# The planner that orders a streaming encoder step estimates a matmul with a larger fixed part and a smaller minimum

## The chip, the cores and the metric

The kernel runs on one core of one Trainium2 chip. The metric is the device time of one execution in microseconds; the median of three runs of the kernel before is 1734.06 us. Engines are named as the profile names them: PE (matmuls), PEld (its weight loads), DVE, ACT, POOL, and SP, which here only issues DMAs.

## The reference

One layer of a hybrid encoder, for 2064 prompt positions (16 learned ones and 2048 given) and 8 short streams of 16 positions that have 256 cached positions each. All is float32.

```python
h = rmsnorm(x, norm_g)
q, k, v, za, logf, bg, u, zc = project(h, w_in, b_f)     # one 1024 x 4104 projection, u = C * h_c
# 8 heads of 64, in blocks of 128 queries; c is the running sum of logf
s = einsum('bqhd,bkhd->bhqk', qblk, k) * DH ** -0.5 + cq - ck
p = softmax(where(kpos <= qpos, s, -inf))
o_a = einsum('bhqk,bkhd->bqhd', p, v)
y_c = bg * causal_conv(u_full, conv_w)                   # depthwise, width 3
x = x + concat(o_a * silu(za), y_c * silu(zc)) @ w_out
y = rmsnorm(x, final_g)                                  # k, v, logf and the last u are outputs too
```

## The kernel before

Every float32 product is made of matmuls on halves: a value is split into a rounded high half and a low remainder (`hh` and `hl` of the normalised tokens, `wh` and `wl` of the weights, `ph` and `pl` of the softmax weights), and three products (high by high, low by high, high by low) add up in PSUM.

**Stages.** Positions are worked on in two groups: 1280 prompt positions with the short streams, and then the other 784. A group is normalised, transposed and projected; its attention runs in between the projections and the convolution, since these need no softmax. Between the two groups the short streams have their own attention, and after the second come the output projection and the last norm.

**A projection** takes a weight of 1024 x 128: `raw` is loaded by a DMA that ACT issues (one buffer), ACT rounds it to `wh`, DVE subtracts to `wl` (two buffers each), and each column tile of the group takes 24 matmuls into a PSUM tile `ps`. A column tile is 256 or 384 wide in the first group and 256 or 272 in the second. Keys and queries leave through the tiles `eh` and `el`, one buffer each (`EB = 1`), and SP stores them to `kh_d`, `kl_d`, `qh_d`, `ql_d` in DRAM.

**Attention** goes by head and by units of 256 queries: five units a head in the first group, three in the second. `scores_of` makes the score tiles `sp` from the query tiles `qa`, `qb` (two of each) and the key tiles `ka`, `kb`, copies them to a row `s` and exponentiates it; `weights_of` transposes the row into `tp` and splits it into `ph` and `pl`; `values_of` adds up `o` (one buffer) from these and from `vb`, the values of the head. `vb` has one buffer, so the load of the next head's values can start only when the last `o` matmul of this head is done. The gate `gz` is multiplied in by POOL, and the result is stored to `cat_d`.

**What sets the order.** All of this is written as generators, the streams `v` (values), `w` (weights), `s` (scores) and the main one (projections or convolution). `weave` steps one of them at a time: the first in the order of priority whose next step has its data by the planner's clock, `self.pe + SLACK`; attention stands ahead of the main stream. That clock is the sum of what `cost` says of every matmul that has been placed, so `cost` sets where attention and projections alternate. PE runs in the order in which the generators were stepped. The orders of DVE, ACT, POOL and SP are sorted by the times that the same planner works out (`note`, `place`, `settle`), and SP issues its DMAs strictly in that order: one that waits holds up those behind it. No instruction is added or left out by `cost`.

```python
                t = s[1]()
                if t <= self.pe + self.SLACK:
                    best = s
                    break
```

Of the kernel before, what the change touches and what calls it, by code (L numbers as in the profile page):

```python
# [67 lines left out]
class Times:  # L68
# [17 lines left out]
    def cost(self, queue, op, out, k):  # L86
        cols = 1
        for x in out.shape[1:]:
            cols *= x
        if queue == "tensor":  # L90
            if op == "transpose":
                return 109.0
            four = k["rhs"].dtype == F32
            return max(214.0 if four else 107.0, cols * (4 if four else 1) / 2.4) + 2.0
        if queue == "gpsimd":
            if k.get("op") == ALU.pow:
                return 464.0
            if op == "partition_all_reduce":
                return 472 + 6.25 * cols
            return 60 + 0.68 * cols if op == "memset" else 115 + 2.2 * cols  # L100
        if queue == "scalar":
            far = k["in_"].tensor.name.rsplit("_", 1)[0] not in WHOLE
            return 52 + 48 * far + 0.83 * cols + 95 * ("accum_out" in k or "bias" in k)
        if op == "tensor_scalar" and "accum_out" in k:
            return 220 + 1.05 * cols
        if op in ("tensor_copy", "tensor_scalar"):
            return 60 + 0.55 * cols + 60 * ("scalar1" in k and not isinstance(k["scalar1"], float))
        if op == "tensor_reduce":
            cols = 1
            for x in k["in_"].shape[1:]:  # L110
                cols *= x
        return 60 + 60 * (op == "scalar_tensor_tensor") + 1.05 * cols

    def place(self, queue, ready, cost):
        if queue == "tensor":
            self.pe = max(self.pe, ready) + cost
            return self.pe
        iv = self.busy.setdefault(queue, [])
        while iv and iv[0][1] < self.pe - 30000.0:
            iv.pop(0)  # L120
        at = max(ready, self.pe - 30000.0)
        k = 0
        while k < len(iv):
            if iv[k][1] > at:
                if iv[k][0] >= at + cost:
                    break
                at = iv[k][1]
            k += 1
        iv.insert(k, (at, at + cost))
        return at + cost  # L130
# [1489 lines left out]
```

## Time and profile before

| what | value |
|---|---|
| median of 3 runs | 1734.06 us (1729.77 to 1741.93) |
| the profiled execution's own time | 1732.57 us |
| its span in the trace | 1730.8 us |
| busy of the span: PE, DVE, ACT, POOL | 91%, 51%, 36%, 13% |
| matmuls | 10311 |
| issued by SP: DMA issues of `vb` | 24, for 16 heads of the two groups |

The profile is of one execution. Its ends of matmuls are modelled, so that the distance between the starts of neighbouring matmuls is what tells a matmul's price, and "idle" of PE is time in which not even the modelled end of a matmul reaches. A time of an instruction in brackets is the idle time of its engine ahead of it, with what ended it.

### The profile page before, as it was taken

Reading aid. Unit: us, or ns where it says so; the run is one execution under the profiler, and the core shown is the slowest. Engines: PE = TensorE matmul, PEld = TensorE weight load, DVE = VectorE, ACT = ScalarE, POOL = GpSimd, SP = SyncE. Lnnn points to the kernel's source line nnn. Section 1 sums busy time; section 2 is a strip of 40 time slices with the busy share of each in tenths; the row PEclk is TensorE's granted clock in tenths of the full one; section 3 lists DMA queues with packets and bytes.
Section 4 is the critical chain, followed back from the end, with each engine's and each line's share of the span. In section 5 each row is a group of like instructions: output and inputs, shape, how many; then the busy total and the mean of one; then the engine's idle time right before and its main releaser. Section 6 shows DMA issues by size and latency. Waiting matters only on the chain.

```text
span 1730.8 us, 27628 instructions
## 1 busy us (share of the span) xinstructions
PE 1578.8 (91%) x10311; PEld 1462.5 (84%) x10311; DVE 881.1 (51%) x2276; ACT 629.2 (36%) x1196; POOL 232.9 (13%) x320
## 2 busy tenths in 40 slices
PE   4977899989889899989995789999999999979998
PEld 4877889989889888989984779989889889968876
DVE  4424566526657566624321547667667657313443
ACT  4323445415435242421110435445545445312111
POOL 2200112100001120121020001000110101112222
PEclk9988999989999999999997889999999999989999
DMA  6454544364542386432136444446533413254443
GB/s 165 161 138 107 136 111 120 99 162 112 138 104 65 108 287 216 131 94 50 42 80 130 110 108 118 120 101 160 129 77 76 104 41 72 64 191 158 130 125 122
DMA packets 222241, 206.03 MB, mean 119 GB/s; under 512 B 26036, under 2 KB 196060, under 8 KB 220444
## 3 DMA queue, kind: packets, MB, share of 16 engines
q1 hardware_dynamic: 160748, 173.34, 34.0%
q10 hardware_dynamic: 61360, 30.94, 10.2%
q8 instruction: 81, 1.33, 0.3%
q14 instruction: 52, 0.43, 0.1%
HBM read 137.28 MB, written 66.93 MB: 118 GB/s over the span
## 4 chain that ended last, share of the span: by engine, by line
PE 59%; DMA 22%; DVE 5%; SPq 4%; issue 3%; ACT 3%; POOL 2%; ACTq 0%; POOLq 0%; DVEq 0%
PE ps L278 33%; PE sp L278 9%; PE o L278 9%; PE tp L278 7%; DMA raw<-in_w_in_dram 4%; SPq L278 4%; DMA cr<-cat_d 4%; DVE oxt L278 2%; DMA vb<-v_d 2%; PE tr L278 2%; DMA qh_d<-eh 1%; DMA qb<-ql_d 1%; DMA kb<-kh_d 1%; DMA gz_d<-kf 1%; DMA sqk_d<-el 1%
## 5 line engine op out<-in xcount | busy, mean ns | idle before, releaser
L278 PE MATMUL ps<-hh,wh 128*128 128x256 f32 (+2 forms) x1568 | 502.7, 321 | 23.6 <-DVE el L278 22.8
L278 PE MATMUL ps<-hl,wh 128*128 128x256 f32 (+2 forms) x1568 | 486.3, 310 | 0.0
L278 PE MATMUL ps<-hh,wl 128*128 128x256 f32 (+2 forms) x1568 | 486.0, 310 | 0.0
L278 PEld LDWEIGHTS ps<-hh,wh 128*128 128x128 f32 x1568 | 302.8, 193 | 34.1 <-DVE el L278 23.9
L278 PEld LDWEIGHTS ps<-hl,wh 128*128 128x128 f32 x1568 | 302.5, 193 | 1.8
L278 PEld LDWEIGHTS ps<-hh,wl 128*128 128x128 f32 x1568 | 301.5, 192 | 0.0
L278 DVE TENSOR_TENSOR pl<-tp,ph 128x512 fp32r<-128x512 f32 (+2 forms) x360 | 199.3, 564 | 121.3 <-ACT ph L278 117.7
L278 ACT CAST ph<-tp 128x512 fp32r<-128x512 f32 (+2 forms) x360 | 171.7, 486 | 224.4 <-PE tp L278 204.6
L278 DVE TENSOR_SCALAR_CACHE_REDUCE s<-sp 128x384 f32<-128x384 f32 (+3 forms) x360 | 211.4, 598 | 50.4 <-PE sp L278 48.8
L278 ACT ACTIVATE s<-s,nm 128x128 f32<-128x128 f32 (+16 forms) x136 | 170.5, 1254 | 84.4 <-DVE nm L278 81.9
L278 PE MATMUL tp<-ident,s 128*128 128x128 f32 (+1 forms) x1224 | 196.4, 272 | 5.0 <-DVE pl L278 5.0
L278 PE MATMUL o<-ph,vb 128*128 128x256 f32 (+4 forms) x584 | 169.8, 310 | 16.5 <-DMA vb<-v_d 11.4
L278 PEld LDWEIGHTS tp<-ident,s 128*128 128x128 f32 (+1 forms) x1224 | 148.5, 142 | 29.1 <-issue 20.9
L278 PE MATMUL sp<-kb,qb 68*128 68x384 f32 (+3 forms) x360 | 144.7, 402 | 24.2 <-DMA qb<-ql_d 20.5
L278 PE MATMUL o<-pl,vb 128*128 128x256 f32 (+4 forms) x584 | 151.2, 285 | 2.0 <-DVE pl L278 1.9
L278 POOL TENSOR_TENSOR gz<-gz,otmp 64x256 f32<-64x256 f32 (+1 forms) x64 | 47.1, 737 | 702.2 <-DVE otmp L278 629.5
L278 PE MATMUL sp<-ka,qa 128*128 128x384 f32 (+3 forms) x360 | 133.7, 371 | 0.0
L278 PEld LDWEIGHTS o<-ph,vb 128*128 128x128 f32 (+1 forms) x584 | 111.7, 191 | 23.9 <-DMA vb<-v_d 12.0
L278 PE MATMUL ps<-o,ch 128*128 128x512 f32 x374 | 118.9, 399 | 11.1 <-ACT ch L278 8.9
L278 PEld LDWEIGHTS o<-pl,vb 128*128 128x128 f32 (+1 forms) x584 | 112.4, 192 | 3.3 <-DVE pl L278 2.6
L278 PEld LDWEIGHTS ps<-o,ch 128*128 128x128 f32 x374 | 70.6, 191 | 29.7 <-ACT ch L278 9.3
L278 DVE TENSOR_TENSOR wl<-raw,wh 128x1024 fp32r<-128x1024 f32 x56 | 69.3, 1238 | 47.5 <-ACT wh L278 47.3
(193 smaller groups left out, 2080.5 us busy)
## 6 DMA issues: line engine op xcount, KB each, us to landing
raw<-in_w_in_dram ACTq DMA_DIRECT2D x59, 512.0 KB
cr<-cat_d SPq DMA_DIRECT2D x17, 512.0 KB
v_d<-vv SPq DMA_DIRECT2D x32, 256.0 KB
vb<-v_d SPq DMA_DIRECT2D x8, 1024.0 KB
oxt<-in_x_prompt_dram SPq DMA_DIRECT2D x16, 512.0 KB
out_dram<-oxt SPq DMA_DIRECT2D x16, 512.0 KB
xt<-in_x_prompt_dram SPq DMA_DIRECT2D x15, 512.0 KB
qa<-qh_d SPq DMA_DIRECT2D x112, 64.0 KB
```

The lines of the kernel that those rows point to most:

```text
L278: r = f(*a, **k)
```

## The change

One line of `cost` for a matmul that isn't a transpose. A matmul of 128 columns counted as 109 ns and counts as 65.3 now; 256 columns 108.7 and 118.7; 272 columns 115.3 and 125.3; 384 columns 162.0 and 172.0; 512 columns 215.3 and 225.3. Transposes stay at 109.

```diff
@@ -91,7 +91,7 @@
             if op == "transpose":
                 return 109.0
             four = k["rhs"].dtype == F32
-            return max(214.0 if four else 107.0, cols * (4 if four else 1) / 2.4) + 2.0
+            return max(214.0 if four else 58.0, cols * (4 if four else 1) / 2.4 + 12.0)
         if queue == "gpsimd":
```

The program holds the same instructions in another order. Three places of it follow, each before and then now.

PE, around the first value matmuls of the first group (the first rows with `o`; `ps` with `wh_1186` is the keys of the second pair of heads, `sp` are scores). Before:

```order
L278 MATMUL ps_1459<-hh1_132,wl_1187 128x384
L278 MATMUL sp_1507<-kb0_1019,qb1_1025 128x384
L278 MATMUL sp_1507<-ka0_1017,qa1_1023 128x384
...
L278 MATMUL sp_1522<-kb0_1019,qb1_1025 128x512
L278 MATMUL sp_1522<-ka0_1017,qa1_1023 128x512
L278 MATMUL sp_1522<-mask_82,identr_83 128x128
L278 MATMUL ps_1531<-hh2_134,wh_1186 128x384
...
L278 MATMUL tr_1538<-ident_77,kf_1514 128x128 x3
L278 MATMUL o_1545<-ph_1345,vb_1021 128x256
L278 MATMUL o_1545<-pl_1346,vb_1021 128x256
```

Now, the same place:

```order
L278 MATMUL sp_1440<-ka0_1017,qa0_1022 128x384
L278 MATMUL sp_1440<-mask_82,identr_83 128x128
L278 MATMUL ps_1430<-hh0_130,wh_1186 128x256
...
L278 MATMUL sp_1459<-kb0_1019,qb1_1025 128x384
L278 MATMUL sp_1459<-ka0_1017,qa1_1023 128x384
...
L278 MATMUL ps_1430<-hh0_130,wl_1187 128x256
L278 MATMUL o_1483<-ph_1332,vb_1021 128x256
L278 MATMUL o_1483<-pl_1333,vb_1021 128x256
```

The first values now stand within the first column tile of those keys (`hh0`) and not within the third (`hh2`): 117 matmuls lay between the first score and the first value matmul, and 91 do now; the first score itself stands 12 matmuls earlier.

SP, around the load of the fifth head's values in the second group (`vb_9636`, two DMAs; `qa`, `qb` are the next unit's queries, `cat_d` the store of the fourth head's last unit). Before:

```order
L278 DMA gz_13512<-gz_d2_113 64x256
L278 DMA qa0_9637<-qh_d2_94 64x272 x2
L278 DMA qb0_9639<-ql_d2_98 64x272
L278 DMA qb0_9639<-c_d_119 1x2x128 x2
L278 DMA cat_d_117<-gz_13114 64x272
L278 DMA vb_9636<-v_d1_109 128x16x128
L278 DMA vb_9636<-v_d1_109 16x128
```

Now:

```order
L278 DMA gz_13293<-gz_d2_113 64x256
...
L278 DMA qh_d3_95<-eh_13180 128x256
L278 DMA ql_d3_99<-el_13182 128x256
L278 DMA vb_9636<-v_d1_109 128x16x128
L278 DMA vb_9636<-v_d1_109 16x128
L278 DMA cat_d_117<-gz_12953 64x272
L278 DMA qa0_9637<-qh_d2_94 64x272 x2
L278 DMA qb0_9639<-ql_d2_98 64x272
L278 DMA qb0_9639<-c_d_119 1x2x128 x2
```

The load of the values now stands ahead of the five query loads and of the store, at this and at the six other head changes of the second group. On PE, 77 to 81 matmuls lay between the last value matmul of a head and the first of the next at these seven places, and 56 to 67 do now, with one of 76.

SP, around the load of the second head's values in the first group (`kh_d`, `kl_d`, `sqk_d` are stores of projected keys out of `eh` and `el`). Before:

```order
L278 DMA vb_1021<-v_d0_108 128x10x128
L278 DMA gz_2030<-gz_d0_111 64x256
L278 DMA qa1_1023<-qh_d0_92 64x256 x2
L278 DMA qb1_1025<-ql_d0_96 64x256
L278 DMA qb1_1025<-c_d_119 1x2x128 x2
L278 DMA qh_d1_93<-eh_2093 128x384
```

Now:

```order
L278 DMA vb_1021<-v_d0_108 128x10x128
L278 DMA kh_d1_101<-eh_1981 128x256
L278 DMA sqk_d_115<-eh_1981 128x128
L278 DMA kl_d1_105<-el_1983 128x256
L278 DMA sqk_d_115<-el_1983 128x128
L278 DMA out_2_dram<-st_2012 128x2x128
```

Stores out of `eh` and `el` now follow this load directly. Before, they followed in that way at the sixth head's load, where now the next queries stand in between; the seventh head's load has stores of queries behind it now too. At the end of the second group, 188 matmuls lay between the last value matmul and the first of the output projection, and 468 do now. The output stage, from its first load on, has one and the same order on SP.

## Rows read from the trace of the kernel before

**Rows 1.** The page's first part: busy time, share of the span, instructions.

```profile
PE 1578.8 (91%) x10311; PEld 1462.5 (84%) x10311; DVE 881.1 (51%) x2276; ACT 629.2 (36%) x1196; POOL 232.9 (13%) x320
```

**Rows 2.** Busy time by stretch, with the granted clock and DMA share.

```profile
core 0: us, PE busy (x) PEld busy (x) DVE busy (x) ACT busy (x) POOL busy (x), PEclk, DMA share, GB/s
0.00:110.00 110.00, 75.46 (x510) 71.69 (x510) 48.97 (x127) 39.60 (x74) 26.31 (x45) 0.95 0.56 147
110.00:590.00 480.00, 438.30 (x2963) 427.90 (x2963) 256.26 (x770) 196.87 (x407) 44.39 (x65) 0.95 0.44 114
590.00:720.00 130.00, 121.81 (x744) 111.93 (x745) 81.44 (x176) 42.77 (x87) 20.30 (x59) 0.96 0.69 227
720.00:965.00 245.00, 204.70 (x1321) 198.50 (x1320) 77.05 (x180) 45.55 (x83) 32.82 (x40) 0.92 0.37 84
...
1050.00:1500.00 450.00, 448.02 (x3267) 408.42 (x3266) 288.98 (x797) 225.00 (x412) 43.57 (x60) 1.00 0.39 94
1500.00:1731.00 231.00, 210.31 (x961) 171.36 (x960) 78.18 (x78) 39.71 (x61) 56.08 (x42) 0.97 0.44 143
```

**Rows 3.** PE's waits: total us, times, longest.

```profile
PE sp L278 <- DMA qb<-ql_d: 20.5, 6, 10.2
...
PE o L278 <- DMA vb<-v_d: 11.4, 4, 8.8
```

**Rows 4.** The chain that ended last, in order of time: start, us, what.

```profile
801.63 60.51 PE ps L278 x381
...
1503.68 13.98 PE ps L278 x114
```

**Rows 5.** PE's timeline: start, us, instruction.

```profile
304.55 0.22 PE L278 MATMUL o<-ph,vb 128*128 128x128 f32 x1
304.61 0.28 PE L278 MATMUL o<-pl,vb 128*128 128x128 f32 x1
...
820.01 0.34 PE L278 MATMUL ps<-hh,wh 128*128 128x384 f32 x1
...
821.05 0.34 PE L278 MATMUL ps<-hh,wh 128*128 128x384 f32 x1
```

**Rows 6.** Timeline at the first scores and values of the first group, PE and SP.

```profile
134.47 0.30 PE L278 MATMUL sp<-kb,qb 68*128 68x128 f32 x1 [1.32 <-DMA qb<-c_d]
...
144.64 0.46 SPq L278 DMA_DIRECT2D vb<-v_d  x1
...
161.43 0.58 PE L278 MATMUL o<-ph,vb 128*128 128x256 f32 x1 [8.82 <-DMA vb<-v_d]
161.81 0.42 PE L278 MATMUL o<-pl,vb 128*128 128x256 f32 x1
```

**Rows 7.** Timeline at the fifth head change of the second group, SP.

```profile
1296.46 1.12 SPq L278 DMA_DIRECT2D qa<-qh_d  x2
...
1300.14 2.51 SPq L278 DMA_DIRECT2D vb<-v_d  x2
```

**Rows 8.** The same place on PE: last value matmul of one head, first of the next.

```profile
1295.52 0.25 PE L278 MATMUL o<-pl,vb 16*128 16x16 f32 x1
...
1307.18 0.36 PE L278 MATMUL o<-ph,vb 128*128 128x256 f32 x1 [0.49 <-DMA vb<-v_d]
```

**Rows 9.** Timeline at the sixth head's load in the first group, SP, ACT, PE.

```profile
436.78 0.53 SPq L278 DMA_DIRECT2D vb<-v_d  x1
437.39 0.62 SPq L278 DMA_DIRECT2D kh_d<-eh  x1
...
447.13 0.38 ACT L278 ACTIVATE eh<-ps 128x256 fp32r<-128x256 f32 x1 [8.10 <-DMA kh_d<-eh]
...
449.33 0.58 PE L278 MATMUL o<-ph,vb 128*128 128x256 f32 x1 [5.16 <-DVE otmp L278]
```

**Rows 10.** The chain's weight loads, start and us.

```profile
31.32 6.51 DMA raw<-in_w_in_dram
...
226.40 10.02 DMA raw<-in_w_in_dram
```

**Rows 11.** Instructions of tile wh: min, median and max ns, first and last start.

```profile
L278 ACT CAST wh<-raw x56: 1034/1049/1074, 28.9 to 1500.3; 128x1024 fp32r<-128x1024 f32 x56
L278 DVE TENSOR_TENSOR wl<-raw,wh x56: 1206/1225/1853, 30.0 to 1502.7; 128x1024 fp32r<-128x1024 f32 x56
```

## The prediction

> **What bounds the kernel now.** I read the page's first part, then the busy time by stage, then what PE waits for. PE is busy for 91% of the span, with DVE next at 51% [rows 1], so the floor is PE's work, and only its waits and a slowed clock can be won or lost. The stages differ [rows 2]. In the second group's attention (1050 to 1500) PE is busy 448.0 of 450 us at a granted clock of 1.00: nothing is to be won there. In the first group's attention (110 to 590) it is busy 438.3 of 480: 41.7 us idle, at a clock of 0.95. Start-up (34.5 us idle of 110), the change of groups (40.3 of 245) and the output stage (20.7 of 231) have waits of their own. The waits that the order could touch end on DMAs: queries 20.5 us in 6 times, values 11.4 us in 4 [rows 3].
>
> **Which estimate is nearer.** Six 384-column matmuls in a row take 821.05 - 820.01 = 1.04 us, 173 ns each [rows 5]; the old table says 162, the new one 172. Two 128-column ones start 60 ns apart [rows 5]; old 109, new 65. The run of 381 at 801.63 takes 158.8 ns a matmul and that of 114 at 1503.68 takes 122.6 [rows 4]; with tiles of 256 and three of 384, and of 256, 256 and 272, the old table gives 148.7 and 110.9, the new one 158.7 and 120.9. So the planner's clock will now be right where it ran 6 to 10% slow. The DMA side of its estimate is left as it was.
>
> A rule speaks against that: the Trainium skill, TensorE: Matmul & The Clock Gate, section Back-to-back issue gap, gives columns/2.4 + 2.5 ns for a warm matmul, which is the old table. The trace differs (173 against 162.5 ns at 384 columns). By the page, a stretch of 58 matmuls would hide some 0.6 us less than I reckon below, so 4 us over the seven head changes would come on top of my sum.
>
> **The change, part by part.** Nothing is added or removed; 10311 matmuls stay, so PE's work is the same to within small changes of neighbours. What moves is attention against projections. A planner's clock that runs faster finds attention's data ready after fewer matmuls, and attention has priority: it stands earlier, with fewer matmuls as cover for every transfer. Before, the slow clock gave each transfer some 8% of cover that nobody planned; that is gone now. The start-up and the output stage keep their orders but for a few rows: 0.
>
> First values. The first score runs at 134.47 and the first value matmul at 161.43, after waiting 8.82 us for `vb`, which SP issued at 144.64 [rows 6]. Without that wait 117 matmuls took 18.1 us, 0.155 each; 91 take 14.1, and the first score stands 12 matmuls (2 us) earlier. PE arrives 6 us sooner at a load that SP issues three rows, about 1.5 us, sooner: the wait grows by 4.5 us. The 4.5 us of projections that slipped behind are cover for later waits on queries, which may give most of it back: between 0 and +6, I take +3, nearer the row's own wait since the later covers shrink too.
>
> The restart after that wait is slow as well: 0.38 us from the first value matmul to the second [rows 6], against 0.12 by the run of 114. It is the half clock (1.2 of 2.4 GHz) that shows in the 0.95; a longer wait pays it no second time, an additional one does, some 1 us.
>
> Stores behind a load. At 436.78 SP issued `vb`, at 437.39 a key store out of `eh`; ACT, which needs `eh` again, sat until 447.13, its queue holds the copy that frees `o`, and PE waited 5.16 us for it [rows 9]. This pattern leaves the sixth head's load and comes to the second and the seventh. One such place more is +5.2; that none bites is -5.2, that both do for long +10. The second head's load already costs PE something now (11.4 less 8.8 us of values' waits are 2.6 at three other places [rows 3]), part of which goes: I take +2.
>
> The Trainium skill, DMA: Bandwidth & Descriptors, section Queues, rings and completion order, says that each DMA engine consumes the descriptors of one ring in order. The row agrees: the store issued 0.6 us behind the load held its buffer for 9.7 us.
>
> Head changes of the second group. 1307.18 - 1295.52 = 11.7 us lie between the values of two heads [rows 8], for 81 matmuls, 0.144 each with the 0.49 wait. The load is issued 4.6 us after the last value matmul, behind five query loads and a store, and lands 7.0 us later [rows 7, 8]. Now 56 to 67 matmuls, 8.1 to 9.6 us, are the cover (76 at one place), but those six DMAs stand behind the load. If it is issued 0.5 us after the last value matmul, it needs 7.5: hidden. Between 0 and the rival below; I take +1 for all seven. What is queued behind the load is the queries of a unit that PE comes to later by more than one unit.
>
> The tail. 468 matmuls, not 188, follow the last values: over six weights in a row with nothing between them. A weight's 72 matmuls take 72 x 122.6 = 8.8 us [rows 4]. The next weight comes round in load + cast + subtract: 6.5 + 1.05 + 1.23 = 8.8 us by the shortest load on the chain, 10.0 + 2.3 = 12.3 by a longer one [rows 10, 11]. With a lead of 8.8 - 2.3 = 6.5 us, five turns at 12.3 lose 5 x 3.5 - 6.5 = 11 us, at 8.8 none. In the tail the DMA queues are calm, so the shorter row is nearer: +0.5.
>
> The short streams and everything else: idle of 8.2 us in 590 to 720 [rows 2], mostly waits for single-buffered loads whose order is shuffled. It can go or double; also the query waits can fall by as much. I take -1, between -8 and +8.
>
> Sum: 3 + 2 + 1 + 0.5 - 1 = +5.5 us on the profiled execution's 1732.57: 1738. That execution lies 1.5 us below the median of the runs, well inside their spread, so I round down to 1737.
>
> **Rivals.** (1) Slower: the value load is late all the same. If the row that SP stands at when the last value matmul is done still waits (a store whose `el` isn't written, say), the old lag of 4.6 us stays, the need is 11.6 us against 8.1 of cover, and six of the seven head changes cost 3.5 us each: +21, with the sum's other terms 1758. It decides from a lag of 1.1 us up. For it: cover was just used up before (0.49 us of wait at the fifth change [rows 8]). Against it: the six DMAs that made the lag stand behind now.
> (2) Faster: right prices place attention better, and half of the 41.7 us of idle in the first group's attention goes: -21, 1712. For it: the planner was wrong by up to a half for 128 columns. Against it: those waits end on DMAs [rows 3], whose estimates stay as they were, and covers there get shorter (70 to 58, 70 to 66, 63 to 55, 58 to 54 matmuls at four head changes).
> (3) The tail becomes bound by weight loads: +11, with the rest 1748. Against it: the calm queues.
> (4) The change does nothing: within 2 us of 1732. The order did move nearly everywhere, but PE's floor holds either way, so this differs from my forecast only in size.
>
> **How the numbers follow.** Forecast with its bounds (1726 to 1748, which takes in rival 4) 0.60; rival 1 or several bad stores 0.16; rival 2 0.16; rival 3 0.08. One per cent (17 us) is about what a measurement of this kernel can tell from no change: faster means under 1717, slower over 1751. Of rival 1 nearly all is slower, of rival 3 a third, of the forecast 0.03: 0.21. Faster: most of rival 2, 0.15. Within: 0.64. The range leaves out a tenth at each side: 1713 to 1759.
>
> **What would show it.** In the new profile: the first value matmul waits 13 us for `vb`; ACT waits for a store out of `eh` behind the second and seventh loads and no more behind the sixth; in the second group SP issues `vb` within 1 us of the last value matmul and PE doesn't wait for it; the stretch of pure projection at the end is some 60 us long and PE idles little in it; PE's idle time in the first group's attention is 42 to 50 us. I am wrong if the idle time in the first group's attention falls below 30 us, or if head changes of the second group show waits of over 2 us.

## The result, and the profile after

The change makes the kernel slower: 1765.53 us, the median of 4 runs (1745.14 to 1767.9), against 1734.85 for the kernel before (1729.77 to 1741.93). The ratio is 1.0151, with a 95% interval of 1.0114 to 1.0188. I had forecast 1737 and a range up to 1759. One of the four executions took 1745.14 us, at a mean granted clock of 0.960; the other three took 1764 us and more, at 0.947 to 0.950.

The profiled execution took 1766.87 us. Its page's first part shows PE's share down by one point and the other engines' busy times within 2 us of those before [rows 1]:

```profile
span 1765.0 us, 27666 instructions
PE 1595.8 (90%) x10311; PEld 1476.6 (84%) x10311; DVE 880.9 (50%) x2276; ACT 631.1 (36%) x1196; POOL 232.0 (13%) x320
```

PE's instructions are the same 10311, yet they are busy for 17 us more. Busy time by stretch shows where. From the second row on I cut the new trace at about the matmuls at which [rows 2] are cut, so that each row holds the same amount of PE's work (stretch, its length, the engines' busy time and instructions, granted clock, DMA share, GB/s):

```profile
0.00:110.00 110.00, 77.25 (x519) 73.65 (x520) 50.04 (x129) 40.26 (x75) 26.06 (x45) 0.95 0.59 154
110.00:587.00 477.00, 434.41 (x2957) 424.63 (x2956) 259.45 (x774) 195.94 (x406) 47.15 (x68) 0.95 0.46 117
587.00:728.00 141.00, 127.43 (x744) 115.88 (x743) 79.02 (x172) 44.59 (x90) 19.43 (x57) 0.91 0.60 194
728.00:977.00 249.00, 203.97 (x1324) 198.02 (x1323) 76.36 (x178) 44.37 (x81) 30.07 (x39) 0.92 0.40 87
...
1053.00:1536.00 483.00, 467.36 (x3263) 422.89 (x3262) 284.14 (x791) 224.04 (x410) 44.71 (x63) 0.95 0.38 88
1536.00:1765.00 229.00, 209.44 (x964) 171.76 (x962) 79.00 (x80) 39.66 (x61) 56.63 (x42) 0.97 0.45 145
```

The first group's attention takes 477 us in place of 480, with 42.6 us of idle time in place of 41.7. The short streams take 141 in place of 130. The second group's attention, of which I had written that nothing is to be won there, is where the time went: its granted clock was 1.00 before [rows 2] and is 0.95 now, and the same matmuls, but for four, take 483 us where they took 450. Its PE is busy 19 us longer and idle 14 us longer. The 85 us ahead of it (965 to 1050 before) became 76, so over the whole group, from matmul 5517 to number 9519, the first of the output projection, it is 595.7 us in place of 571.4: 24.3 of the 34.2 us between the two spans.

PE's waits in that stretch are few (who waited for whom, us in total, times, longest):

```profile
PE tp L278 <- DVE pl L278: 9.4, 4, 4.8
PE ps L278 <- DVE kf L278: 3.0, 2, 1.7
PE o L278 <- DMA vb<-v_d: 1.7, 1, 1.7
PE ps L278 <- ACT kf L278: 1.6, 1, 1.6
```

Finer stretches around the waits for `pl` tell the rest:

```profile
1062.00:1142.00 80.00, 79.98 (x579) 71.13 (x577) 53.05 (x160) 42.09 (x77) 7.55 (x14) 1.00 0.46 115
1142.00:1146.00 4.00, 0.00 (x0) 0.00 (x0) 0.04 (x1) 0.46 (x2) 0.00 (x0) 0.71 0.57 161
1146.00:1164.00 18.00, 17.21 (x65) 13.98 (x66) 7.43 (x18) 4.91 (x13) 0.00 (x0) 0.50 0.15 41
1164.00:1217.00 53.00, 50.43 (x375) 46.72 (x374) 33.95 (x98) 28.04 (x48) 2.23 (x3) 1.00 0.54 123
1217.00:1239.00 22.00, 21.20 (x82) 16.88 (x82) 7.61 (x20) 5.06 (x15) 0.00 (x0) 0.54 0.12 33
1239.00:1292.00 53.00, 50.11 (x370) 46.30 (x369) 34.21 (x97) 28.91 (x47) 4.64 (x4) 1.00 0.62 162
1292.00:1304.00 12.00, 12.00 (x53) 9.77 (x54) 4.40 (x11) 3.07 (x8) 0.63 (x1) 0.58 0.30 46
```

PE does nothing from 1142 to 1146. In the 18 us behind that it runs 65 matmuls at a granted clock of 0.50, the lower of its two levels (1.2 of 2.4 GHz), where 18 us at full clock held some 130. The wait cost 4.8 us and the slow matmuls behind it some 9. At 1217 a wait of 1.7 us is followed by 20.5 us at half clock, at 1292 one of 2.5 by 10.2. (These lengths are read from the trace's record of the granted clock; the clock of a stretch is the mean over it.) In a row of busy shares such a stretch looks like work: PE is busy throughout, only for twice as long.

The timeline at the first of these places shows whom PE waited for (SP, ACT and PE; start, us, instruction, idle time before it and what ended it):

```profile
1131.14 1.68 SPq L278 DMA_DIRECT2D ka<-kh_d  x1
1132.91 0.54 SPq L278 DMA_DIRECT2D ka<-kl_d  x1
1133.50 1.79 SPq L278 DMA_DIRECT2D kb<-kh_d  x1
...
1138.56 0.34 SPq L278 DMA_DIRECT2D qh_d<-eh  x1
...
1145.54 0.38 ACT L278 ACTIVATE eh<-ps 128x256 fp32r<-128x256 f32 x1 [6.36 <-DMA qh_d<-eh]
1145.82 0.67 ACT L278 CAST ph<-tp 128x272 fp32r<-128x272 f32 x2
...
1146.79 0.90 PE L278 MATMUL tp<-ident,s 128*128 128x128 f32 x3 [4.80 <-DVE pl L278]
```

SP issued a head's load (`ka`, `kb`) at 1131 to 1135 and a store out of `eh` at 1138.56. ACT, which wanted `eh` for the next queries, sat until 1145.54. Behind that instruction in ACT's queue stood two casts of `ph`, which attention needed, and PE waited for what is made from them. This is [rows 9] again, in the other group. The Trainium skill, DMA: Bandwidth & Descriptors, section Queues, rings and completion order, says that descriptors of one ring are taken in order; the trace agrees, with a store of 128 KB that held its buffer for 7.0 us behind 1.5 MB of loads.

ACT's waits for DMAs in the same stretch name the other places:

```profile
ACT wh L278 <- DMA raw<-in_w_in_dram: 10.3, 3, 3.8
ACT kf L278 <- DMA cat_d<-kf: 7.2, 1, 7.2
ACT eh L278 <- DMA qh_d<-eh: 6.4, 1, 6.4
ACT eh L278 <- DMA kh_d<-eh: 2.7, 1, 2.7
```

The second store out of `eh` led to the wait at 1217, a wait of 3.8 us for a weight load to that at 1291.9. That load isn't queued behind SP's: ACT issues it, and its 0.52 MB moved on another queue (q10), beside 2.40 MB of SP's queue (q1), most of it the next head's keys. It was issued at 1273.88, and ACT could use it at 1289.18 (1272 to 1290; packets, MB, share of the DMA engines' time):

```profile
q1 hardware_dynamic: 1620, 2.40, 58.1%
q10 hardware_dynamic: 1040, 0.52, 15.4%
```

Before the change the second group had one such place, in the stretch 965 to 1050, which my rows had left out. A store out of `kf` was issued at 1012.51, behind a head's `ka` and `kb` (1005.79 to 1011.14); ACT waited 6.13 us for it, PE 4.59, and 10.2 us at half clock followed:

```profile
1024.13 0.40 ACT L278 ACTIVATE kf<-ps 128x272 f32<-128x272 f32 x1 [6.13 <-DMA gz_d<-kf]
1027.12 0.90 PE L278 MATMUL tp<-ident,s 128*128 128x128 f32 x3 [4.59 <-DVE pl L278]
```
```profile
1027.00:1037.00 10.00, 9.88 (x37) 7.75 (x38) 4.22 (x14) 2.35 (x7) 0.91 (x2) 0.51 0.34 92
```

### The profile page after: what moved, and what is told of

It is laid out like the page before. It is cut to its first block, busy times and chain, and to the rows that moved or that the text cites. A ratio compares the mean times of both kernels' runs of the same rounds, so it can differ in the third digit from the quotient of the medians.

```text
span 1765.0 us, 27666 instructions
## 1 busy us (share of the span) xinstructions
PE 1595.8 (90%) x10311; PEld 1476.6 (84%) x10311; DVE 880.9 (50%) x2276; ACT 631.1 (36%) x1196; POOL 232.0 (13%) x320
## 4 chain that ended last, share of the span: by engine, by line
PE 56%; DMA 18%; DVE 5%; issue 3%; ACT 3%; SPq 2%; POOL 1%; ACTq 0%; POOLq 0%; DVEq 0%
PE ps L278 30%; PE o L278 9%; PE sp L278 8%; PE tp L278 7%; DMA cr<-cat_d 3%; SPq L278 2%; DVE oxt L278 2%; DMA qh_d<-eh 2%; DMA raw<-in_w_in_dram 2%; DMA vb<-v_d 2%; PE tr L278 1%; DMA oraw<-in_w_out_dram 1%; DMA kb<-kh_d 1%; ACT osq L278 1%; DMA gz_d<-kf 1%
## 5 line engine op out<-in xcount | busy, mean ns | idle before, releaser
L278 PE MATMUL tp<-ident,s 128*128 128x128 f32 (+1 forms) x1224 | 201.3, 277 | 9.4 <-DVE pl L278 9.4
L278 PEld LDWEIGHTS tp<-ident,s 128*128 128x128 f32 (+1 forms) x1224 | 150.6, 144 | 37.1 <-issue 23.9
L278 PE MATMUL o<-ph,vb 128*128 128x256 f32 (+4 forms) x584 | 174.0, 317 | 8.1 <-DVE otmp L278 4.3
L278 PEld LDWEIGHTS o<-pl,vb 128*128 128x128 f32 (+1 forms) x584 | 115.3, 197 | 1.2 <-DVE pl L278 0.6
L278 PEld LDWEIGHTS sp<-kb,qb 68*128 68x128 f32 (+1 forms) x360 | 66.9, 186 | 43.9 <-issue 28.7
```

The lines of the kernel that those rows point to most:

```text
L278: r = f(*a, **k)
```

## The experiments

"Before" in each comparison is the kernel before, run beside it; its medians were 1738.0 (first four kernels), 1735.7 (the next four) and 1737.3 (the last four).

**By stage and by part of the formula.** A: dearer matmuls mean fewer of them as cover for each transfer. B: the loss begins in the short streams; B' (the same letter in two of the expectations): the smaller minimum does it. C, later called D: each new order throws new dice.

`late`: the new estimate from the second group's attention on (the diff is shortened).

```diff
-            return max(214.0 if four else 107.0, cols * (4 if four else 1) / 2.4) + 2.0
+            return NEW if self.new else OLD     # the two formulas
-        self.attention_tiles(1, self.open(ctx, "ap1", side="right"))
+        self.nc.new = True; self.attention_tiles(1, self.open(ctx, "ap1", side="right"))
```

> The new estimate only from the second group's attention on; all before it is planned as before. Theory A (the loss sits in the second group's attention, where transfers have lost cover): 1757 us, 1750 to 1765, that is +15 to +30. Theory B (the loss comes from the short streams and what is handed on from there): 1735 to 1740. Theory C (any new order throws new dice): anything from 1730 to 1770, and the waits stand at other places than after the whole change.

Measured: 1750.08 us, ratio 1.0093 (1.0060 to 1.0127). At the foot of A's range and out of B's. The place of the loss is confirmed: PE waits 4.55 us at 1138.8, where the whole change waits at 1146.8, with the same 20.5 us at half clock behind it. C had the waits at other places; they are at the same ones.

From matmul 5104 on (869.5 us in after's trace) `late` and after have one and the same order on every engine. Yet `late` is 10 us (by the ratios) to 15 us (by the medians) faster, and its second group takes 584.3 us in its trace, after's 595.7. They part at the second bad place. ACT waits 1.9 us for the store there and PE 0.9, where after has 2.7 and 1.7, and the clock stays full, where after has 20.5 us at half clock:

```profile
1208.25 0.60 PE L278 MATMUL tp<-ident,s 128*128 128x128 f32 x3 [0.88 <-DVE pl L278]
```
```profile
1208.00:1229.00 21.00, 20.75 (x139) 17.98 (x140) 12.93 (x38) 9.03 (x20) 0.77 (x1) 1.00 0.39 102
```

So one order has no single price: against before's 571.4 us, this one costs the second group 13 us in one trace and 24 in the other.

`early`: the same switch the other way round, `True` from the start and `False` from that line on.

> The new estimate only up to the second group's attention, the old one from there. Theory A: 1743 us, 1736 to 1750 (7 us won in the first group's attention, 15 lost in the short streams, a few in the norm and projections behind them). Theory B: 1755 to 1768. Theory C: anything from 1730 to 1770.

Measured: 1737.17 us, ratio 0.9997 (0.9979 to 1.0016). In A's range (1736 to 1750) and out of B's. By itself the new order of the first 5100 matmuls is worth nothing either way. With it ahead of the new second group, after is slower than `late`; whether by chance (after has four executions, and one at 1745) or by what it hands on, no run here shows. The 11 us that the profile of after loses in the short streams are in part that run's own: from matmul 3470 to 4462, with the same order, they took 182.0, 177.2 and 175.7 us in three executions, with the old one 168.5 to 175.0 in seven (`late` and those of the kernels below that keep it).

`fixed` and `minim`: one part of the new formula each.

```diff
-            return max(214.0 if four else 107.0, cols * (4 if four else 1) / 2.4) + 2.0
+            return max(214.0 if four else 109.0, cols * (4 if four else 1) / 2.4 + 12.0)   # fixed
+            return max(214.0 if four else 58.0, cols * (4 if four else 1) / 2.4) + 2.0     # minim
```

> The larger fixed part alone: columns/2.4 + 12, at least 109, so only matmuls of 256 columns and more get dearer. Theory A (cover lost because long matmuls are priced higher): 1755 to 1768. Theory B' (it is the smaller minimum of the 128-column score matmuls that pulls attention ahead): 1730 to 1740.

> The smaller minimum alone: 128-column matmuls at 60 in place of 109, all others as before. Theory A: 1728 to 1740, since nothing gets dearer and every transfer keeps its cover in matmuls or gains some. Theory B': 1755 to 1768.

Measured: `fixed` 1768.44, ratio 1.0191 (1.0160 to 1.0222); `minim` 1762.99, ratio 1.0154 (1.0104 to 1.0204). Each half alone costs as much as the whole. A expected the first and is refuted by the second: there no matmul got dearer, and the second group is slower all the same. (Those of 256 columns got 0.3 ns cheaper too: with the minimum of 107 they counted 109.0 before, not the 108.7 given with the change.) Only C takes both, though its range, 1730 to 1770, is so wide that little could have spoken against it.

**How sensitive the order is.** Three kernels change nothing but the 2.0 of the old formula, and only from the second group's attention on: 3.0 (`tiny_p1`), -1.0 (`tiny_m2`), 5.0 (`tiny_p3`).

```diff
-            return max(214.0 if four else 107.0, cols * (4 if four else 1) / 2.4) + 2.0
+            return max(214.0 if four else 107.0, cols * (4 if four else 1) / 2.4) + (3.0 if self.new else 2.0)
```

> The kernel before, with every matmul priced 1 ns higher (+3 in place of +2) from the second group's attention on. Theory D (every new order of the second group throws new dice, and the order before was a lucky throw): 1743 to 1768, with waits at places of its own. Theory A (what counts is how much dearer the matmuls get): 1732 to 1740, as before.

> The kernel before, with every matmul priced 3 ns lower (-1 in place of +2) from the second group's attention on. Theory D (any new order costs, whichever way the price goes): 1743 to 1768. Theory A (dearer matmuls cost cover, cheaper ones give it): 1728 to 1736.

> The kernel before, with every matmul priced 3 ns higher (+5 in place of +2) from the second group's attention on. Theory D: 1743 to 1768, and not ordered by the price: it may lie below the kernel with 1 ns (1749). Theory A: a little above the kernel with 1 ns, 1750 to 1756, on the way to the whole change.

Measured: +1 ns 1749.12, ratio 1.0091 (1.0060 to 1.0123); -3 ns 1752.31, ratio 1.0096 (1.0067 to 1.0126); +3 ns 1728.16, ratio 0.9943 (0.9915 to 0.9972). So a price that differs by 1 ns costs over half of what the whole change costs, a lower price costs the same, and a higher one makes the kernel faster than before. A is out by all three. D's range (1743 to 1768) holds two of them; the third lies 15 us below it, so D holds in part: a new order may also win, and the order before wasn't the best throw, only a good one. In the second group of the +1 ns kernel PE waits for `pl` as it does after the whole change, here because ACT stood 6.0 us for a store out of `kf` and 7.0 us for a weight load:

```profile
PE tp L278 <- DVE pl L278: 11.6, 4, 5.4
PE o L278 <- DMA vb<-v_d: 1.0, 1, 1.0
```

In that of the +3 ns kernel (960 to 1510) one wait of over 0.6 us is left, the one at the group's start that the other kernels have too, and from 970 to 1510 PE is busy for 539.13 of 540 us at full clock:

```profile
PE tr L278 <- ACT kf L278: 11.6, 1, 11.6
PE o L278 <- ACT ph L278: 0.5, 1, 0.5
```
```profile
970.00:1510.00 540.00, 539.13 (x3940) 493.48 (x3939) 337.27 (x941) 266.81 (x488) 58.81 (x77) 1.00 0.41 100
```

**More cover.** `lat1900_after` is the kernel after with one number of the planner changed.

```diff
-DMA_LATENCY = 1350.0
+DMA_LATENCY = 1900.0
```

> The kernel after, with the planner's end of every transfer 550 ns later (1900 in place of 1350), which gives each transfer three to five matmuls of cover back. Theory A (the change took cover away): 1734 to 1745. Theory D (new dice, with an order as good or bad as others): 1743 to 1768.

Measured: 1739.99, ratio 1.0013 (0.9979 to 1.0047). The time is A's; in the second group the reason isn't. Most of the gain over after came ahead of it. The group's attention began (matmul 5517) at 953.3 us against 972.5 there and 960.7 before, which is 19 of the 25 us between the spans of the two profiled executions. I didn't take these 19 apart; after's order ahead of the second group reached that matmul at 963.1 and 966.5 in two other traces, so up to 9 of them are that execution's own. In the second group, where A wanted the waits gone, ACT still stands 5.2 us behind a store out of `eh` and 4.5 for a weight load; PE waits 3.3 and 3.5 us for it, with 13.7 us at half clock behind each. Without the trace this run would have passed for a proof of A.

```profile
ACT wh L278 <- DMA raw<-in_w_in_dram: 13.5, 4, 4.6
...
ACT eh L278 <- DMA qh_d<-eh: 5.2, 1, 5.2
```

**The cause by itself.** The next three leave every engine's order as it is in after or before (in `eb_before` but for the issue of one weight load at 204 us): the planner still reckons with the old buffers, only the tiles that it hands out are more. A fourth, `stall`, adds instructions to ACT's order alone. Theory Q: a DMA that ACT needs is queued behind a head's load, PE waits for ACT, and the half clock follows. T: only the idle time counts. N: the stores have nothing to do with it.

```diff
-        t = self.pool.tile(shape, dtype, name=name, bufs=bufs)
+        t = self.pool.tile(shape, dtype, name=name, bufs={"eh": 2, "el": 2, "nm": 10}.get(name, bufs) if self.times.second else bufs)
```

(`eh` and `el` are 272 columns wide in the second group there, and `nm` has 10 buffers in place of 16, so that all fits in SBUF.)

> The kernel after, with the same order on every engine, but two buffers each for eh and el in the second group (the planner still reckons with one). Theory Q (ACT stands behind a store of eh that is queued behind a head's load, PE waits for ACT, and each such wait brings the half clock): the two waits at 1146.8 and 1217.8 (4.8 and 1.7 us) go, and with them the 41 us at half clock behind them (worth some 20): 1742 us, 1736 to 1750. Rival T (only the idle time itself counts, the half clock comes anyway): 1760. Rival N (the stores have nothing to do with it): 1766.

> The same second buffers in the kernel before, as a control. In its second group ACT hardly waits for stores of eh: by all theories 1732 to 1738. If it is faster by over 5 us, two buffers are worth something by themselves and the result after is to be read against it.

Measured: `eb_after` 1747.11, ratio to before 1.0065 (1.0044 to 1.0087), where after has 1.0151; `eb_before` 1733.25, ratio 0.9979 (0.9951 to 1.0007). 18 us between the medians are gone with two buffers and no other edit, of which the idle time was 6.5. The times alone don't refute T and N: `late`, with the same order of the second group and one buffer, has 1750.08. In the traces the second group takes 581.5 us with two buffers, 14 less than in after and 3 less than in `late`. What refutes them is the two places, where the waits and the half clock behind them are gone. In the timeline of `eb_after`, ACT's writes of `eh` at that place start without a wait:

```profile
1133.94 0.39 ACT L278 ACTIVATE eh<-ps 128x256 fp32r<-128x256 f32 x1
...
1142.99 0.40 ACT L278 ACTIVATE eh<-ps 128x272 fp32r<-128x272 f32 x1 [0.44 <-PE ps L278]
```

The rest of what after loses to before is still there: the wait for the weight load, and a new one for `vb`, which is why the gain isn't larger. PE's waits of that kernel from 976 to 1300, the weight load's behind `pl` and one for `vb`, are followed by 17.1 and 6.8 us at half clock:

```profile
PE o L278 <- DMA vb<-v_d: 5.3, 1, 5.3
PE tp L278 <- DVE pl L278: 3.2, 1, 3.2
```

`kf3` takes the one wait for a store out of the kernel before: the planner reckons with two buffers for `kf`, and every third of the first twelve tiles comes from a third (the lines of the diff that matter).

```diff
+        if name == "kf" and self.times.third and self.times.nkf < 12:
+            self.times.nkf += 1
+            if self.times.nkf % 3 == 0:
+                pool, shape = self.times.third, [P, 272]
```

> The kernel before with the same order, and a third buffer for kf in the first four projections of the second group (the planner still reckons with two). Before, ACT waits there 6.1 us at 1024 for a store out of kf, PE 4.6 us for ACT, and 10.2 us at half clock follow. Theory Q: wait and half clock go: 1726 us, 1721 to 1731. Rival T (only the wait counts): 1731. Rival N (it moves to the next wait): 1735.

Measured: 1728.60, ratio 0.9957 (0.9926 to 0.9988), 8.7 us below the median of before: near Q's size, but the interval (2 to 13 us) takes in T's 1731 too, so the time alone doesn't decide. The traces do: the stretch of the table below is 7.5 us shorter than before's, more than the 4.6 us of the wait itself. In its trace ACT writes `kf` without a wait for the store, and PE is busy for all of the 20 us around it at full clock:

```profile
1020.63 0.40 ACT L278 ACTIVATE kf<-ps 128x272 f32<-128x272 f32 x1 [0.44 <-PE ps L278]
```
```profile
1010.00:1030.00 20.00, 20.00 (x136) 16.84 (x135) 9.36 (x25) 9.12 (x23) 0.91 (x2) 1.00 0.76 161
```

`stall` puts such waits in. It is the kernel before with useless copies of 8 columns behind the 120th, 220th, 320th and 420th of ACT's instructions in the second group.

```diff
                 todo.append((self.times.key, len(todo), r.ins))
+                for _ in range(STALL.pop(self.times.nact, 0)):    # {120: 20, 220: 34, 320: 48, 420: 70}
+                    todo.append((self.times.key, len(todo), self.engine.copy(out=self.times.idle[0], in_=self.times.idle[1]).ins))
```

> The kernel before with the same order, and with 20, 34, 48 and 70 useless small copies put into ACT's queue at four places of the second group's attention (some 2, 3.5, 5 and 7 us). Theory Q (a wait of PE of some 2 us and more costs its own time and then 10 to 20 us at half clock): 1760 us, 1750 to 1772: about 11 us of waits and 5 to 10 us of half clock behind each of the longer ones. Rival T (waits cost only themselves): 1742 to 1748.

Measured: 1782.32, ratio 1.0254 (1.0200 to 1.0308), 47 us above before. The copies took over twice what I had reckoned, 34 of them 7.75 us, so both numbers of the expectation are too low. PE's waits show the share of each: 1.35, 6.53, 8.07 and 14.19 us, 30.1 in all; behind them 0, 23.9, 10.2 and 17.1 us at half clock. T with the true waits would be some 1766 (1735.7 + 30.1); the missing 16 us are the slow matmuls, as part of the half clock lies in the waits themselves. At the second place (ACT's copies, then busy time ahead of the wait, in it, behind it):

```profile
1219.58 7.75 ACT L285 COPY idle<-ident 128x8 f32<-128x8 f32 x34
```
```profile
1205.00:1223.00 18.00, 18.00 (x133) 16.19 (x132) 9.77 (x32) 10.57 (x30) 0.74 (x1) 1.00 0.91 229
1223.00:1230.00 7.00, 0.47 (x5) 0.27 (x4) 1.70 (x3) 5.27 (x22) 0.00 (x0) 0.83 0.86 268
1230.00:1251.00 21.00, 21.00 (x81) 17.02 (x82) 5.89 (x16) 5.24 (x13) 2.35 (x1) 0.50 0.12 27
```

Here a busy ACT is enough to make PE wait, and the half clock follows; no store has to be late for it.

**All fourteen kernels by one sum.** The part from matmul 5560 to the end of the last matmul ahead of the output projection holds the same work in every kernel (but for two of its 3959 matmuls). From its length I take PE's waits of over 0.5 us, and half of the time at half clock that lies outside them (in which PE did half of its work):

| kernel | length, us | waits | at half clock | left |
|---|---|---|---|---|
| tiny_p3 | 543.3 | 0.5 | 0 | 542.8 |
| kf3 | 547.1 | 2.2 | 0 | 544.9 |
| early | 554.4 | 5.9 | 10.2 | 543.6 |
| before | 554.6 | 5.2 | 10.2 | 544.5 |
| eb_before | 558.9 | 7.2 | 17.1 | 543.5 |
| eb_after | 564.7 | 11.9 | 23.9 | 541.9 |
| late | 567.7 | 12.5 | 30.7 | 541.2 |
| tiny_p1 | 569.6 | 12.7 | 34.1 | 540.8 |
| lat1900_after | 570.5 | 15.9 | 27.3 | 541.4 |
| tiny_m2 | 573.2 | 16.2 | 37.5 | 541.2 |
| after | 579.1 | 15.3 | 51.2 | 539.7 |
| fixed | 580.1 | 20.4 | 34.1 | 543.6 |
| minim | 582.8 | 26.2 | 37.5 | 541.4 |
| stall | 598.1 | 34.6 | 61.4 | 541.2 |

The lengths differ by 55 us, what is left by 5. What is left falls as the half clock grows (by a straight line through the fourteen, some 0.08 us for each us of it outside the waits), so half of the slow time is a little too high a price for it. In the second group the order matters by its waits and by the clock that follows them, and by nothing else that these traces show. The Trainium skill, TensorE: Matmul & The Clock Gate, section Terms, reckons a slow clock's cost in the same way, the time spent slow times the share of the clock that is missing; the last column agrees with it to within these 5 us.

## Why the prediction was wrong, step by step

Neither of the signs by which I had said I would be wrong came: the first group's idle time didn't fall, and no head change of the second group waited for over 2 us. Both looked where the loss wasn't. The chance of 0.16 for rival 1 took in "several bad stores"; bad stores did come, but in the other group and at another price.

**Failed: the price of a wait.** I wrote that an additional wait pays the half clock too, "some 1 us". It was read from the distance of two matmuls behind a wait (0.38 us in place of 0.12, [rows 6]) as if the next ones ran at full speed again. The trace of before spoke against it at that very place, where 16 matmuls in 5 us ran at the lower level:

```profile
161.00:166.00 5.00, 4.57 (x16) 4.09 (x17) 2.57 (x7) 2.35 (x5) 0.00 (x0) 0.50 0.50 158
166.00:172.00 6.00, 6.00 (x45) 5.96 (x44) 4.14 (x14) 2.91 (x6) 1.45 (x2) 0.97 0.21 56
```

Measured: 20.5, 20.5 and 10.2 us at half clock behind the three waits of after, a loss of some 9, 10 and 5, where the waits themselves are 4.8, 1.7 and 2.5. By the table, after has 10.1 us more of waits than before and loses 19.3 more by the clock, less 4.8 by which what is left is shorter: the 24.5 us between the two lengths. In `kf3` the clock is worth 4.8 us and the waits 3.0, in `eb_after` against after 13.2 and 3.4.

**Failed: stores behind a load, +2 (-5 to +10).** The pattern was right and read from the right row; I looked for it in the first group alone, where the trace of before showed it, and let it bite at one place more at most. Two of the three places in after are stores out of `eh` behind a head's load in the second group. Their waits and half clock come to some 25 us in after's trace, partly through the price above; `eb_after`, where they are gone and others came, has 18 us less by the medians and 14 in the second group's trace. In the first group, where I looked, the pattern cost next to nothing: ACT's wait of 8.1 us behind the sixth load is gone, as I said, but behind the second load it is 0.9 us and behind the seventh there is none; one of 8.2 us at 357 was there before too.

**Failed: the direction.** "Fewer matmuls as cover" was the mechanism from which every sign of mine came. With -3 ns the kernel is as slow as with +1, and with +3 faster than before; `minim` makes nothing dearer and loses 1.5%. What decides is which store falls behind a head's load, and which weight load beside one. In the second group a new order had little to win, since the old one had a single bad place; that nothing is to be won there was nearly right (`kf3` and `tiny_p3` win 8.7 and 9.2 us, most of it at that place), but I took it for "nothing happens there".

**First values, +3.** Wrong in its mechanism; that the size is near is luck. I expected a wait of 13 us for `vb`; SP issued it 2.6 us earlier than before and the first value matmul found it there. Waits for queries came in its place, 3.3 us at 130.9 and 7.6 at 162.6 (SP, PE):

```profile
142.09 0.39 SPq L278 DMA_DIRECT2D vb<-v_d  x1
...
147.23 0.28 PE L278 MATMUL o<-ph,vb 128*128 128x256 f32 x1
...
162.57 0.66 PE L278 MATMUL sp<-kb,qb 68*128 68x384 f32 x1 [7.61 <-DMA qb<-ql_d]
```

The stage's idle time, 42.6 us, is in the band that I gave (42 to 50), and `early` shows what the new order comes to up to the second group's attention: nothing.

**Head changes of the second group, +1.** Right for this order: `vb` is issued within half a microsecond of the last value matmul, and PE waited for it once, 1.7 us, without a fall of the clock. Rival 1 isn't dead for that: `minim` waits 8.4 us for `vb`, `tiny_m2` 7.6, `eb_after` 5.3.

**Tail, +0.5 (0 to +11).** Three waits of 1.3, 1.7 and 1.6 us, behind ACT's waits for two weight loads (2.8 and 3.7 us) and for a store out of `kf` (7.2): +4.6, and the clock stayed full. Rival 3's mechanism, within the term's bounds.

**Everything else, -1 (-8 to +8).** The profile shows +11 in the short streams; `early`, which has their order, is no slower than before.

**Which estimate is nearer.** The new table is nearer to the trace, as I said: 384 columns take 173 ns from start to start [rows 5]. The rule that I set against it is the old table only from 256 columns up; at 128 the old table had 109 ns. A nearer table is worth nothing here: what hurts is a DMA's time behind or beside another's, which neither table touches.

Open remains how to find a good order without trying: I haven't shown a change of the planner that avoids these places, only buffers that remove them and prices that happen to.

## What to carry to other kernels

When an edit re-deals the order of a stretch that is busy throughout at full clock, the stretch can only stay or lose. Each new wait of some microseconds there cost its own time in these runs and then, mostly, 2 to 12 us more in slow matmuls: price both. Ask of every store whether the buffer that it empties is wanted again soon, by an engine that others wait for, and whether a long load is queued ahead of it; here a second buffer at such a place won time, and the better estimate none. Before a change of a planner's number is credited or blamed, change the number by a nanosecond: if that moves the time by as much, it is the throw that was measured and not the number. And look at more than one execution: `late` and after have the same order where they lose, and the losses are 13 and 24 us.

## What the runs showed of the hardware that I had not expected

The half clock follows short waits. Over the fourteen traces of the second group (the part that the table takes), 28 of 30 waits of 2.2 us and more were followed by 3.4 to 24 us at half clock, and one of 45 waits between 0.5 and 1.7 us; its length doesn't go with the wait's (1.7 us was followed by 20.5, 14.2 by 17.1). At one place of the same order, a wait of 0.9 us in `late` was followed by none and one of 1.7 us in after by 20.5.

A copy of 8 columns on ACT took 197 ns in the median of 172, and 34 in a row 7.75 us, 228 each.

One and the same order reached matmul 4462, ahead of the second group's norm, between 753.8 and 764.0 us in eight profiled executions, so one trace of a stage with many DMA waits is good to some 10 us.
